# A two-layer encoder trunk in fp32 halves: a changed planner, more load slots, and a new opening with the first norm's weights transposed by PE

## The chip, the core and the metric

The kernel runs on one core of a Trainium2 chip. The metric is the device time of one execution in microseconds. Five engines work side by side, each through its own instructions in order: PE (matrix products and transposes into PSUM), ACT (activations, copies and casts), DVE (elementwise work and reductions), POOL (elementwise work on SBUF only) and SP, which here only issues the DMAs.

## The reference

The input is one sequence of 256 tokens with 1024 features. Two layers follow, each of a SwiGLU feed-forward block, a mixer and a second feed-forward block, every one of them with a norm ahead and a norm behind. All data are fp32.

```python
def rmsnorm(x, g):
    y = x * lax.rsqrt(jnp.mean(x * x, axis=-1, keepdims=True) + EPS)
    return y * g
def swiglu(h, wg, wu, wd):            # 1024 -> 2816 -> 1024
    return (jax.nn.silu(h @ wg) * (h @ wu)) @ wd
for l in range(2):
    g = norm_g[l]
    x = x + 0.5 * rmsnorm(swiglu(rmsnorm(x, g[0]), wg[l, 0], wu[l, 0], wd[l, 0]), g[1])
    h = rmsnorm(x, g[2])
    m = even_mixer(h, ...) if l == 0 else odd_mixer(h, ...)
    x = x + rmsnorm(m, g[3])
    x = x + 0.5 * rmsnorm(swiglu(rmsnorm(x, g[4]), wg[l, 1], wu[l, 1], wd[l, 1]), g[5])
```

The even mixer projects 1024 features to 3368, applies rotary tables, runs 4 differential attention heads and 8 heads that attend to the 64 best of the keys by an indexer's score, and projects back. The odd mixer projects to 3072, runs 16 heads with a bias from a table of clipped distances, and projects back.

## The kernel before

**Tiles.** The tokens are two row blocks of 128, X[0] and X[1] (t = 0 and 1 in the code). Every operand of a matmul is held as a high and a low part in a reduced fp32 type (wh and wl for weights, xTh and xTl for the transposed activations, blk for hidden values), and a product is three matmuls: high by high, high by low and low by high. So each weight that is loaded (tile raw, 512 KB, four slots) is cast by ACT to wh (L267) and reduced by DVE to wl = raw - wh (L269), in pieces of 512 columns.

**Blocks.** A feed-forward block takes its 2816 hidden columns in chunks, one of 256 (tok) and five of 512: gate and up projections into PSUM banks called ps, SiLU on ACT (L532), the product on DVE (L541), transposes by PE (L388), and the down projection into banks called y. A block ends with postnorm: squares of y on ACT (L471), y times g on DVE (L476), the root on POOL (L408, L410), the update of X on DVE (L482). Then prenorm makes the next input: X times g on DVE (L425), squares on ACT (L429), transposes on PE (L388), xTh on ACT (L346), xTl on DVE (L352). The first norm has its own form, prenorm0: X is transposed as it is, and the copies out of PSUM scale by g, which is held as a column per partition (gT), on ACT (L348) and DVE (L354).

**Mixers.** In the even mixer the rotary step takes three DVE operations out of PSUM (L630, L634) and one addition of two SBUF tiles on POOL (L637); the indexer accumulates its scores on DVE (L811) and picks maxima (L818, L819); softmax runs over L705, L709 and L732, the scores' matmuls are L688, the values' L738 to L740. In the odd mixer a table of biases per group of heads comes by DMA (L975).

**Order.** All work is first recorded in a list: every entry has an engine, an estimated time, its inputs and outputs, and a position. Positions follow PE's main stream (pl.pos counts the main matmuls' time); weights stand 9 us ahead of their use (LEAD). Plan.issue then plays an event simulation with these estimates and hands out, for each engine that is free, the ready entry with the lowest position whose buffers are free. The instructions are written in the order in which this hands them out, so a change of an estimate, a slot count or a position moves instructions on all engines. Two rules matter here: an entry with the mark "port" (two SBUF inputs on DVE, or any work of POOL) starts only when the last such one has ended, and its engine stands idle until then (L153 to L156); and a PE entry counts as ready only 0.6 us (SAFE) after its last input from another engine (L164).

**Opening.** SP loads X[0], then g as 1024 single elements (L302), then the first weights and X[1]. Six matmuls of zeros (WARM) keep PE at work until X is there.

## Time and profile before

| | us |
|---|---|
| median of 3 runs | 1026.03 (1025.42 to 1026.78) |
| the profiled execution, its own time | 1024.73 |
| its span | 1022.3 |
| PE busy | 1000.7 (98%) |
| PE weight loads busy | 845.3 (83%) |
| DVE busy | 657.3 (64%) |
| ACT busy | 548.1 (54%) |
| POOL busy | 43.7 (4%) |
| HBM, mean rate over the span | 180 GB/s |

The profile is of one execution; its span runs from the first to the last instruction. A busy PE may run at full clock (2.4 GHz, 1.00 in the rows) or at half (1.2 GHz, 0.50), which the busy time does not tell apart. An idle time is put down to what came last before the instruction behind it.

### The profile page before, as it was taken

The page shows a single profiled execution, that of the slowest core. Times are in us where ns is not written, and L with a number is a line of the kernel's source. Part 1 is how long each engine was busy: PE and PEld are TensorE (multiplying, and loading weights), DVE is VectorE, ACT ScalarE, POOL GpSimd, SP SyncE. Part 2 cuts the span into 40 slices and gives each one's busy share as a digit, 9 for nine tenths or more (in the row PEclk, how much of TensorE's full clock was granted, in tenths as well). Part 3 has the DMA queues.
Part 4 walks back from the last instruction along what each step waited for, and adds up shares of the span by engine and source line. Part 5 has one row for each costly group of instructions (what it writes and reads, how often), then busy time and mean ns, then how long its engine had stood idle before and what let it go on. Part 6 is the DMA issues. An engine that isn't in the chain of part 4 may idle for free.

```text
span 1022.3 us, 14425 instructions
## 1 busy us (share of the span) xinstructions
PE 1000.7 (98%) x5166; PEld 845.3 (83%) x5166; DVE 657.3 (64%) x1299; ACT 548.1 (54%) x1134; POOL 43.7 (4%) x80
## 2 busy tenths in 40 slices
PE   8999999999998999999999999999999989999997
PEld 8888888887876988888888888888899878888886
DVE  6755555689999565545477545557678777555552
ACT  7644444557568454544366444455467756444441
POOL 1000000120200000000010000000000010000000
PEclk8999999999999999999999999999999999999999
DMA  8965665463445476665467666654784347656631
GB/s 286 292 190 181 191 186 163 134 227 105 165 126 163 149 243 185 189 186 198 128 206 246 189 185 187 193 195 147 215 246 155 104 145 230 192 180 194 192 125 41
DMA packets 94151, 185.45 MB, mean 181 GB/s; under 512 B 7040, under 2 KB 29440, under 8 KB 94080
## 3 DMA queue, kind: packets, MB, share of 16 engines
q1 hardware_dynamic: 94080, 184.54, 57.6%
q8 instruction: 40, 0.66, 0.2%
q14 instruction: 31, 0.25, 0.1%
HBM read 183.47 MB, written 1.05 MB: 180 GB/s over the span
## 4 chain that ended last, share of the span: by engine, by line
PE 93%; DVE 3%; ACT 2%; DMA 1%; issue 1%; SPq 0%; POOLq 0%; DVEq 0%; POOL 0%; ACTq 0%
PE ps L378 14%; PE ps L379 14%; PE ps L380 14%; PE y L378 9%; PE y L380 9%; PE y L379 9%; PE ps L370 6%; PE ps L371 5%; PE ps L373 5%; PE ps L388 4%; PE ps L688 1%; DVE wl L269 1%; DMA raw<-in_ow_in_dram 1%; ACT wh L267 1%; DMA raw<-in_wg_dram 0%
## 5 line engine op out<-in xcount | busy, mean ns | idle before, releaser
L269 DVE TENSOR_TENSOR wl<-raw,wh 128x512 fp32r<-128x512 f32 (+1 forms) x664 | 427.6, 684 | 273.2 <-ACT wh L267 272.1
L267 ACT CAST wh<-raw 128x512 fp32r<-128x512 f32 (+1 forms) x664 | 378.6, 617 | 318.6 <-PE ps L380 170.7
L378 PE MATMUL ps<-wh,xTh 128*128 128x512 f32 x592 | 230.4, 389 | 0.0
L380 PE MATMUL ps<-wh,xTl 128*128 128x512 f32 x592 | 230.3, 389 | 0.0
L379 PE MATMUL ps<-wl,xTh 128*128 128x512 f32 x592 | 230.3, 389 | 0.0
L378 PE MATMUL y<-wh,blk 128*128 128x512 f32 x352 | 139.1, 395 | 0.0
L380 PE MATMUL y<-wh,blk 128*128 128x512 f32 x352 | 137.2, 390 | 0.0
L379 PE MATMUL y<-wl,blk 128*128 128x512 f32 x352 | 137.0, 389 | 0.0
L380 PEld LDWEIGHTS ps<-wh,xTl 128*128 128x128 f32 x592 | 111.1, 188 | 23.1
L378 PEld LDWEIGHTS ps<-wh,xTh 128*128 128x128 f32 x592 | 111.1, 188 | 23.0
L379 PEld LDWEIGHTS ps<-wl,xTh 128*128 128x128 f32 x592 | 111.1, 188 | 23.0
L370 PE MATMUL ps<-wh,xTh 128*128 128x512 f32 (+2 forms) x320 | 110.6, 360 | 4.5 <-ACT xTh L346 3.1
L371 PE MATMUL ps<-wl,xTh 128*128 128x512 f32 (+2 forms) x320 | 107.8, 351 | 0.0
L380 PEld LDWEIGHTS y<-wh,blk 128*128 128x128 f32 x352 | 66.1, 188 | 13.9
L379 PEld LDWEIGHTS y<-wl,blk 128*128 128x128 f32 x352 | 66.2, 188 | 13.0
L378 PEld LDWEIGHTS y<-wh,blk 128*128 128x128 f32 x352 | 66.1, 188 | 12.9
L370 PEld LDWEIGHTS ps<-wh,xTh 128*128 128x128 f32 x320 | 62.8, 196 | 12.5 <-ACT xTh L346 3.9
L371 PEld LDWEIGHTS ps<-wl,xTh 128*128 128x128 f32 x320 | 63.1, 197 | 6.1
L373 PE MATMUL ps<-wh,xTl 128*128 128x512 f32 (+2 forms) x320 | 66.5, 347 | 0.0
L388 PE MATMUL ps<-ident,t 128*128 128x128 f32 x386 | 55.9, 273 | 5.7 <-DVE t L425 2.3
L388 PEld LDWEIGHTS ps<-ident,t 128*128 128x128 f32 x386 | 45.5, 140 | 16.2 <-issue 5.6
L373 PEld LDWEIGHTS ps<-wh,xTl 128*128 128x128 f32 x320 | 52.1, 193 | 6.7
(120 smaller groups left out, 938.2 us busy)
## 6 DMA issues: line engine op xcount, KB each, us to landing
raw<-in_wu_dram SPq DMA_DIRECT2D x88, 512.0 KB, 4.3
raw<-in_wd_dram SPq DMA_DIRECT2D x88, 512.0 KB, 3.4
raw<-in_wg_dram SPq DMA_DIRECT2D x86, 512.0 KB, 3.8
raw<-in_ew_in_dram SPq DMA_DIRECT2D x24, 512.0 KB, 4.3
raw<-in_ow_in_dram SPq DMA_DIRECT2D x24, 512.0 KB, 4.6
g<-in_norm_g_dram SPq DMA_DIRECT2D x11, 512.0 KB, 5.1
raw<-in_ew_out_dram SPq DMA_DIRECT2D x8, 512.0 KB, 4.4
raw<-in_ow_out_dram SPq DMA_DIRECT2D x8, 512.0 KB, 3.8
```

The lines of the kernel that those rows point to most:

```text
L267: nc.scalar.copy(ref.t[0][:, sl], raw.t[:, sl])
L269: nc.vector.tensor_sub(ref.t[1][:, sl], raw.t[:, sl], ref.t[0][:, sl].bitcast(F32))
L370: nc.tensor.matmul(o(), ah, bh, start=k == 0, stop=False)
L371: nc.tensor.matmul(o(), ah, bl, start=False, stop=False)
L373: nc.tensor.matmul(o(), al, bh, start=False, stop=k == KT - 1)
L378: nc.tensor.matmul(o, ah, bh, start=start, stop=False)
L379: nc.tensor.matmul(o, ah, bl, start=False, stop=False)
L380: nc.tensor.matmul(o, al, bh, start=False, stop=stop)
L388: nc.tensor.transpose(b.t[:, k * P:(k + 1) * P], s[:, k * P:(k + 1) * P], ident.t)
L688: nc.tensor.matmul(bs[h].t[:, QS[t]], q()[i][rs, bq, t * P:(t + 1) * P], KB.t[j][rs, bk, 0:KL[t]], start=i + j == 0, stop=i == 1)
```

## The change

Six things change.

- Slots: raw has six instead of four; small tiles 14 instead of 16.
- Planner: an entry with the port mark is passed over while the port is taken, so its engine takes other ready work. The 0.6 us of margin for PE is no longer waited for: an entry without margin is only taken if none with margin is ready; entries that take PE's results get the same margin. DMA is estimated at 315 instead of 360 GB/s. An entry may name two engines, and goes to the one that is free first.
- Work that may go to DVE or POOL: the weight subtractions of the even mixer (all projections but the indexer's and the first) and of its output projection, those of the first up projection, and the rotary additions.
- Norms: the work of postnorm and prenorm on ACT and DVE stands 9 us earlier in position. The last down and output projections of each block run column half by column half. Two multiplications of 512 columns behind the differential heads become eight ACT copies of 128.
- Opening, loads: X[0] first half, g as 8 rows of 128 into a tile of the mask, X[0] second half, the first gate weights in four parts, then the up weights and X[1].
- Opening, work: PE transposes g (one matmul, a DVE copy to gT), X[0]'s transposes go to two banks each, copies of X and casts of the first gate weights (now 256 columns each) take turns, the squares of X come behind the copies, and two matmuls of zeros (FILL) follow X[0]'s transposes.

```diff
-SLOTS = {"raw": 4, "w": 8, "xT": 2, "t2": 7, "blk": 8, "g": 2, "pt": 2, "ps": 4, "y": 4, "sm": 16}
+SLOTS = {"raw": 6, "w": 8, "xT": 2, "t2": 7, "blk": 8, "g": 2, "pt": 2, "ps": 4, "y": 4, "sm": 14}
-LAT = {"PE": 0.2, "ACT": 0.14, "DVE": 0.13, "POOL": 0.17, "DMA": 2.0}
+LAT = {"PE": 0.2, "ACT": 0.14, "DVE": 0.13, "POOL": 0.17, "DMA": 2.2}
-WARM = 6
+WARM, FILL = 6, 2
...
+                    if o["port"] and port > now + 1e-9:
+                        fits = False
+                        event(port, "", None)
...
-                    if fits:
+                    if fits and o["safe"] <= now + 1e-9:
                         got = o
                         break
+                    if fits and late is None:
+                        late = z
...
-                    d["ready"] = max(d["ready"], end + (OWN[e] if d["eng"] == (e,) else o["lat"] + (SAFE if d["eng"] == ("PE",) else 0.0)))
+                    at = end + (OWN[e] if d["eng"] == (e,) else o["lat"])
+                    d["ready"] = max(d["ready"], at)
+                    if d["eng"] == ("PE",) != (e,):
+                        d["safe"] = max(d["safe"], at + SAFE)
...
-            self.step = 512 if self.per * b % 512 == 0 else b
+            self.step = 512 if self.per * b % 512 == 0 and (pool or first is None) else b
...
-                op(DVE, n_dve(self.step), lo, r=[rk, (ref, i, 0)], w=[(ref, i, 1)], pos=q + 0.05, port=True)
+                op(DVE + POOL if self.pool else DVE, {"DVE": us, "POOL": 0.1 + self.step * 0.00245} if self.pool else us, lo,
+                   r=[rk, (ref, i, 0)], w=[(ref, i, 1)], pos=q + 0.05, port=True)
...
-    op(DMA, 0.1, lambda: nc.sync.dma_start(gT.t, norm_g[0, 0].rearrange("(k p) -> p k", p=P)), w=[gT], pos=-99.5)
+    op(DMA, 0.1, lambda: nc.sync.dma_start(cmask.t[0:KT, 0:P], norm_g[0, 0].rearrange("(k p) -> k p", p=P)), w=[cmask], pos=-100)
+    op(PE, 0.11, lambda: nc.tensor.transpose(bb.t[:, P:P + KT], cmask.t[0:KT, 0:P], ident.t[0:KT, 0:KT]), r=[cmask, ident], w=[bb], pos=-90)
+    op(DVE, 0.08, lambda: nc.vector.tensor_copy(gT.t, bb.t[:, P:P + KT]), r=[bb], w=[gT], pos=-90)
...
+        first = pos - LEAD
...
+        pos = pl.pos - LEAD
...
+        order = [(k, t, n) for k in range(kn) for t in ts for n in range(2)]
+        if last:
+            order.sort(key=lambda o: o[2])
...
-        op(POOL, 0.11 + n * 0.00218, lambda: nc.gpsimd.tensor_add(a.t[:, :n], a.t[:, :n], r.t[:, :n]),
+        op(DVE + POOL, {"DVE": n_dve(n), "POOL": 0.11 + n * 0.00218}, add, r=[(r, 0), (r, 1)], w=[a], port=True)
...
-            op(DVE, n_dve(512), scl, r=[(ss, 4), oA[t]], w=[(jk, h) for h in range(4)], pos=pn)
+                op(ACT, n_act(P, True, 1), scl, r=[(ss, 4), oA[t]], w=[(jk, h)], pos=pn)
```

The order at the opening, on SP (loads). X0 and X1 are the row blocks, raw the weights' slots. Before:

```order
L291 DMA X0_72<-in_x_dram 128x512 x2
L302 DMA gT_74<-in_norm_g_dram 128x8x1
L259 DMA raw_2_106<-in_wg_dram 128x2x256
L291 DMA X1_73<-in_x_dram 128x512 x2
L259 DMA raw_2_106<-in_wg_dram 128x2x256
```

And now:

```order
L303 DMA X0_72<-in_x_dram 128x512
L315 DMA cmask_75<-in_norm_g_dram 8x128
L303 DMA X0_72<-in_x_dram 128x512
L269 DMA raw_2_107<-in_wg_dram 128x2x256 x2
L269 DMA raw_5_119<-in_wg_dram 128x2x256 x2
L269 DMA raw_12_142<-in_wu_dram 128x2x256 x2
L303 DMA X1_73<-in_x_dram 128x512 x2
```

X1's two loads stood behind the first of the weights' loads and stand behind the sixth now.

The order at the opening, on ACT (xTh are copies out of PSUM, wh weight casts, t2 the squares of X). Before:

```order
L454 ACTIVATE t2_4_113,sm_3_112<-X0_72 128x512
L454 ACTIVATE t2_5_117,sm_3_112<-X0_72 128x512
L348 ACTIVATE xTh_8_131<-ps_6_120,gT_74 128x128
L267 CAST wh_10_135<-raw_2_106 128x512
L348 ACTIVATE xTh_8_131<-ps_6_120,gT_74 128x128 x3
L348 ACTIVATE xTh_8_131<-ps_7_126,gT_74 128x128 x4
L267 CAST wh_10_135<-raw_2_106 128x512
```

And now:

```order
L365 ACTIVATE xTh_8_129<-y_3_113,gT_74 128x128
L365 ACTIVATE xTh_8_129<-y_4_114,gT_74 128x128 x2
L277 CAST wh_10_138<-raw_2_107 128x256 x2
L365 ACTIVATE xTh_8_129<-y_3_113,gT_74 128x128
L277 CAST wh_10_138<-raw_2_107 128x256 x2
L365 ACTIVATE xTh_8_129<-y_6_123,gT_74 128x128
L277 CAST wh_14_160<-raw_5_119 128x256
L365 ACTIVATE xTh_8_129<-y_7_124,gT_74 128x128
L277 CAST wh_14_160<-raw_5_119 128x256
```

The squares have moved behind the copies, and each later copy has a cast of half the size behind it.

The order on POOL where the even mixer begins (t2 tiles are rotary results). Before:

```order
L637 TENSOR_TENSOR t2_332_1912<-t2_332_1912,t2_335_1923 128x288
L783 COPY t2_332_1912<-t2_332_1912 128x96
L637 TENSOR_TENSOR t2_336_1935<-t2_336_1935,t2_339_1953 128x512
L637 TENSOR_TENSOR t2_359_2044<-t2_359_2044,t2_360_2048 128x288
L783 COPY t2_359_2044<-t2_359_2044 128x96
```

And now:

```order
L816 COPY t2_339_1942<-t2_339_1942 128x96
L279 TENSOR_TENSOR wl_355_2021<-raw_323_1854,wh_354_2020 128x512
L279 TENSOR_TENSOR wl_358_2031<-raw_331_1897,wh_357_2030 128x512
L670 TENSOR_TENSOR t2_362_2054<-t2_362_2054,t2_365_2061 128x288
L279 TENSOR_TENSOR wl_364_2059<-raw_338_1928,wh_363_2058 128x512
L816 COPY t2_362_2054<-t2_362_2054 128x96
L279 TENSOR_TENSOR wl_376_2100<-raw_361_2046,wh_375_2099 128x512
```

Weight subtractions have come to POOL, 35 in the whole program, and of ten rotary additions three are left there, two of 512 columns and one of 288.

The order on ACT where the even mixer hands over to the feed-forward block (y tiles are the mixer's output, X0 the updated row block, xTh the next input). Before:

```order
L471 ACTIVATE t2_617_3350,sm_616_3349<-y_531_2943 128x512
L471 ACTIVATE t2_618_3355,sm_616_3349<-y_534_2952 128x512
L267 CAST wh_621_3370<-raw_606_3287 128x512 x2
L471 ACTIVATE t2_624_3379,sm_623_3378<-y_554_3041 128x512
L429 ACTIVATE t2_626_3383,sm_625_3382<-X0_72 128x512
L429 ACTIVATE t2_628_3387,sm_625_3382<-X0_72 128x512
L267 CAST wh_630_3391<-raw_613_3318 128x512 x2
L471 ACTIVATE t2_634_3409,sm_623_3378<-y_559_3057 128x512
L346 CAST xTh_635_3412<-ps_632_3396 128x4x128
```

And now:

```order
L500 ACTIVATE t2_622_3372,sm_621_3371<-y_550_3020 128x512
L500 ACTIVATE t2_625_3386,sm_621_3371<-y_557_3040 128x512
L500 ACTIVATE t2_628_3399,sm_627_3398<-y_582_3158 128x512
L277 CAST wh_629_3405<-raw_603_3257 128x512 x2
L447 ACTIVATE t2_632_3411,sm_631_3410<-X0_72 128x512
L447 ACTIVATE t2_634_3415,sm_631_3410<-X0_72 128x512
L500 ACTIVATE t2_637_3424,sm_627_3398<-y_585_3174 128x512
L363 CAST xTh_640_3436<-ps_636_3419 128x4x128
```

The two casts that stood between the squares of X0 and the copy to xTh are gone from there.

## Rows read from the trace of the kernel before

**Rows 1.** The page's busy times: share of the span and number of instructions of each engine.

```profile
PE 1000.7 (98%) x5166; PEld 845.3 (83%) x5166; DVE 657.3 (64%) x1299; ACT 548.1 (54%) x1134; POOL 43.7 (4%) x80
```

**Rows 2.** Busy time of each engine in stretches of 20 us, with the granted clock of PE (1.00 is 2.4 GHz), the share of the DMA engines and GB/s.

```profile
0.00:20.00 20.00, 16.25 (x92) 15.24 (x93) 12.25 (x32) 14.92 (x39) 3.54 (x13) 0.83 0.88 274
...
200.00:220.00 20.00, 19.29 (x108) 16.76 (x107) 18.02 (x41) 12.54 (x25) 4.55 (x8) 1.00 0.72 240
...
240.00:260.00 20.00, 18.11 (x114) 14.05 (x113) 19.68 (x77) 12.00 (x36) 0.00 (x0) 1.00 0.35 108
...
300.00:320.00 20.00, 19.34 (x124) 16.09 (x123) 19.04 (x67) 17.68 (x51) 0.00 (x0) 1.00 0.53 156
320.00:340.00 20.00, 16.37 (x94) 14.17 (x93) 16.36 (x31) 10.70 (x28) 4.52 (x8) 0.91 0.60 192
...
740.00:760.00 20.00, 18.45 (x148) 17.70 (x148) 14.52 (x40) 12.51 (x32) 0.89 (x3) 0.91 0.85 269
...
820.00:840.00 20.00, 17.41 (x107) 14.99 (x106) 16.60 (x31) 11.87 (x29) 4.50 (x8) 1.00 0.54 168
```

**Rows 3.** The same in two stretches of the opening; the figure behind POOL's is the granted clock.

```profile
8.00:10.00 2.00, 1.54 (x8) 1.04 (x6) 1.83 (x7) 2.00 (x7) 0.00 (x0) 0.65 1.04 368
...
14.00:16.00 2.00, 2.00 (x13) 2.00 (x13) 2.00 (x6) 2.00 (x6) 0.00 (x0) 0.64 0.78 237
```

**Rows 4.** The timeline of the opening: start, duration (of a run of like instructions their whole time), engine, line, operation, and the idle time before it with what ended it.

```profile
5.17 0.35 ACT L348 ACTIVATE xTh<-ps,gT 128x128 fp32r<-128x128 f32 x1
...
6.32 0.62 ACT L267 CAST wh<-raw 128x512 fp32r<-128x512 f32 x1 [0.80 <-DMA raw<-in_wg_dram]
6.84 1.91 ACT L348 ACTIVATE xTh<-ps,gT 128x128 fp32r<-128x128 f32 x7
...
6.99 1.37 PE L388 MATMUL ps<-ident,X 128*128 128x128 f32 x8 [1.47 <-DMA X<-in_x_dram]
...
7.75 0.87 DVE L354 SCALAR_TENSOR_TENSOR xTl<-ps,gT,xTh 128x128 fp32r<-128x128 f32 x3
...
8.77 0.55 PE L370 MATMUL ps<-wh,xTh 128*128 128x256 f32 x1 [0.41 <-ACT xTh L348]
...
10.66 0.55 PE L370 MATMUL ps<-wh,xTh 128*128 128x256 f32 x1 [0.70 <-DVE xTl L354]
...
12.93 2.48 DVE L269 TENSOR_TENSOR wl<-raw,wh 128x512 fp32r<-128x512 f32 x4
```

**Rows 5.** Busy times, as in rows 2, around the longest wait of the even mixer.

```profile
236.00:250.00 14.00, 12.11 (x70) 9.06 (x69) 13.75 (x44) 8.38 (x23) 0.65 (x1) 1.00 0.41 127
```

**Rows 6.** The timeline of the even mixer: a POOL addition beside DVE work, the indexer's accumulation on DVE without and with a POOL addition beside it, and PE's longest wait.

```profile
220.78 2.21 POOL L637 TENSOR_TENSOR t<-t,t 128x512 f32<-128x512 f32 x1 [0.36 <-DVE t L634]
...
229.07 0.34 DVE L811 SCALAR_TENSOR_TENSOR t<-t,wI,cmask 128x128 f32<-128x128 f32 x1
229.29 1.29 POOL L637 TENSOR_TENSOR t<-t,t 128x512 f32<-128x512 f32 x1 [6.30 <-DVE t L634]
229.44 1.28 DVE L811 SCALAR_TENSOR_TENSOR t<-t,wI,t 128x128 f32<-128x128 f32 x1
...
248.16 0.55 PE L388 MATMUL ps<-ident,t 128*128 128x128 f32 x3 [1.63 <-DVE blk L354]
```

**Rows 7.** The timeline where the even mixer hands over to the feed-forward block.

```profile
320.85 3.09 DVE L269 TENSOR_TENSOR wl<-raw,wh 128x512 fp32r<-128x512 f32 x5
...
324.76 0.50 PE L380 MATMUL y<-wh,xTl 128*128 128x512 f32 x1 [1.09 <-DVE xTl L352]
...
330.22 1.13 ACT L267 CAST wh<-raw 128x512 fp32r<-128x512 f32 x2
...
332.45 0.39 PE L370 MATMUL ps<-wh,xTh 128*128 128x256 f32 x1 [1.43 <-ACT xTh L346]
```

**Rows 8.** Busy times and granted clock, as in rows 2, behind the waits at 332 and at 749 us.

```profile
332.00:336.00 4.00, 3.55 (x18) 3.55 (x19) 3.68 (x8) 0.89 (x2) 1.47 (x4) 0.61 0.57 148
...
749.00:752.00 3.00, 3.00 (x17) 3.00 (x17) 2.65 (x15) 2.72 (x10) 0.31 (x1) 0.55 1.05 278
752.00:755.00 3.00, 3.00 (x25) 3.00 (x25) 1.89 (x4) 1.85 (x5) 0.31 (x1) 0.88 1.00 322
```

**Rows 9.** The odd mixer: busy times of two stretches, as in rows 2 (the last two figures are the share of the DMA engines and GB/s).

```profile
724.00:728.00 4.00, 4.00 (x19) 3.30 (x19) 2.37 (x4) 3.02 (x6) 0.00 (x0) 1.00 0.00 0
...
740.00:744.00 4.00, 4.00 (x35) 4.00 (x35) 1.85 (x3) 2.28 (x4) 0.27 (x1) 1.00 0.99 346
```

**Rows 10.** The chain that ended last, at the load of the odd mixer's weights (start, duration).

```profile
738.80 7.06 DMA raw<-in_ow_in_dram
```

**Rows 11.** PE's waits in the timeline, in the odd mixer and where it hands over to the feed-forward block.

```profile
747.12 0.33 PE L688 MATMUL ps<-KBh,blk 64*128 64x128 f32 x2 [1.03 <-ACT KBh L346]
...
827.23 1.23 PE L388 MATMUL ps<-ident,t 128*128 128x128 f32 x8 [1.16 <-DVE t L425]
...
829.89 0.39 PE L370 MATMUL ps<-wh,xTh 128*128 128x256 f32 x1 [1.43 <-ACT xTh L346]
```

**Rows 12.** The timeline of the tail: PE's last matmul, the last square and the last update.

```profile
1015.85 0.39 PE L380 MATMUL y<-wh,blk 128*128 128x512 f32 x1
...
1016.27 0.60 ACT L471 ACTIVATE t<-y 128x512 f32<-128x512 f32 x1
...
1017.90 1.54 DVE L482 SCALAR_TENSOR_TENSOR X<-t,sm,X 128x512 f32<-128x512 f32 x3 [0.21 <-POOL sm L410]
```

More of the change, by code (lines that the diff above doesn't have):

```diff
@@ L124, in issue @@
                     continue
-                skip, got = [], None
+                skip, got, late = [], None, None
                 while heap[e]:
@@ L137, in issue @@
                             event(q.used[1], "", None)
-                    if fits:
+                    if fits and o["safe"] <= now + 1e-9:
                         got = o
                         break
+                    if fits and late is None:
+                        late = z
                     skip.append(z)
+                if got is None and late is not None:
+                    got = late[2]
+                    skip.remove(late)
                 for z in skip:
@@ L149, in issue @@
                     q.t = q.make()
-                us = o["us"]
-                o["fn"]()
-                start = now
+                us = o["us"] if len(o["eng"]) == 1 else o["us"][e]
+                o["fn"]() if len(o["eng"]) == 1 else o["fn"](e)
                 if o["port"]:
-                    start = max(start, port)
-                    port = start + us
-                end = eng[e] = o["end"] = start + us
+                    port = now + us
+                end = eng[e] = o["end"] = now + us
                 todo -= 1
@@ L425, in mg @@
                     nc.vector.tensor_mul(xn[h].t, X[t].t[:, HS[h]], g.t[:, HS[h]])
-                op(DVE, n_dve(512), mg, r=[(X[t], h), (g, h)], w=[xn[h]], pos=pos - 0.01, port=True)
+                op(DVE, n_dve(512), mg, r=[(X[t], h), (g, h)], w=[xn[h]], pos=first - 0.01, port=True)
             q = t2() if late else xn[h]
@@ L488, in down, with f @@
     def down(ts, unit, kn, lhs, lk, y, kt0, first, last):
[L490 to L497 removed]
+        order = [(k, t, n) for k in range(kn) for t in ts for n in range(2)]
+        if last:
+            order.sort(key=lambda o: o[2])
+        for k, t, n in order:
+            wk, w = unit.part(k, n * 512, (n + 1) * 512)
+            def f(n=n, k=k, w=w, t=t):
+                mm3(y[t][n].t, tuple(z[:, kt0 + k, t * P:(t + 1) * P] for z in lhs()), w(),
+                    first and k == 0, last and k == kn - 1)
+            main(0.68, f, r=wk + lk(t), w=[y[t][n]])
     last_silu = [None]
```

91 lines of the change are left out of this document (48 added, 43 removed).

## The prediction

> **What bounds the kernel now.** I read the page's first line before anything else: PE is busy for 1000.7 of the span's 1022.3 us [rows 1], so only what PE loses can move the end. Next the busy time in stretches of 20 us [rows 2]: the feed-forward stages fill PE and are left out there; the losses sit in the opening (3.75 us idle in 0 to 20), in the even mixer (0.71, 1.89 and 0.66 in three stretches), where it hands over to the next feed-forward block (3.63 in 320 to 340), in the odd mixer (1.55 in 740 to 760) and at its handover (2.59 in 820 to 840). The rest of the idle time is the tail behind the last matmul and two gaps below half a microsecond. Last the granted clock, which the busy time hides: it is 2.4 GHz nearly everywhere, but 1.2 GHz in the opening from about 8.6 to 15.4 us (a mean of 0.65 over 8 to 10 is 1.4 us at half, 0.64 over 14 to 16 the same) [rows 3], and for some 3.4 us each after the waits at 332 and 749 [rows 8]. At half clock PE counts as busy and does half the work, so 3.4 us there lose 1.7 us.
>
> **The change part by part.** I count gains against the profiled execution (1024.73 us, 2.43 above its span); its median is 1.30 higher, and I carry the difference over.
>
> Opening. The load of the first norm's weights shrinks from 1024 elements of 4 bytes to 8 rows, X's second row block and its load go behind the first weights, and casts of X and of weights alternate. The first scaled copy of X was at 5.17 [rows 4]; it still needs four transposes, and now one more on PE and a DVE copy, so I leave it there. A copy of 128 columns takes ACT 0.27 (1.91 for 7) and DVE 0.29 (0.87 for 3); a weight cast of 512 columns takes 0.62 on either (0.62; 2.48 for 4), so I put one of 256 at 0.33, half and a little [rows 4]. Eight copies and eight casts are 4.8 us on ACT and 5.0 on DVE, which starts one copy later: done at about 10.7. PE follows them from about 6.6 on (5.17, three copies, a cast, the low part's subtraction; the first weights had landed by 6.32 even behind the small elements), so by 10.7 it has run the first 16 weight matmuls, against 5 before, when it waited 0.41 and 0.70 and got going at 10.66 [rows 4]. That is 11 matmuls, 0.21 us each at 1.2 GHz, 2.3 us; but eight transposes of X's second block, which before were done (1.37 us, within an idle stretch) now stand in the stream. Net 0.9. I take 0.7. Upper end: if the earlier matmuls and the two filling ones keep the clock up, the 6.8 us at half clock go, 3.4. Lower end: thinner work before 10.7 puts the rise of the clock off by one stretch like those of rows 8, so -1.7 + 0.7 = -1.0. Casts and loads cannot limit PE after that: the 0.5 MB of X are moved behind 1.5 MB of weights, and PE wants X's second block only after 24 matmuls.
>
> Here the Trainium skill speaks against the change: its page TensorE: Matmul & The Clock Gate (Part 4, PE-mode transpose) says that transposes do not count as PE work for the clock. By that, the transposes now in the stream would put the rise off, and the opening would give -1.0; the trace agrees so far as the clock fell at 8.6 right behind the transposes of 6.99, but they also followed a wait of 1.47 [rows 4].
>
> Even mixer. DVE is the second engine here: 13.75 busy of 14 us around PE's longest wait, 1.63 at 248.16 [rows 5, 6]. By the program's order 35 weight subtractions (0.62 each) leave DVE for POOL, 21.7 us; seven rope additions come back, at most 4.2; two scalings go to ACT, where time is free. So DVE loses about 17 us of work in a stage of 120. But a POOL addition of two tiles takes 1.29, and DVE work on two SBUF tiles beside it waits: an accumulation of 0.34 took 1.28; the other way round POOL took 2.21 [rows 6]. The planner now lets neither start while the other holds the port and takes other work instead. The waits of this stage sum to 3.26 [rows 2]; I take 1.0 of it, between all of it and a loss of 3 (below): a relief that is real, on a path which PE waits for only now and then.
>
> Even to feed-forward. Before, five weight subtractions (3.09 us) stood ahead of the last head's low part, for which PE waited 1.09 [rows 7]. Now three do: two less, 1.2 us earlier. Against it, the last output projection runs its column halves one after the other, so one more group (three matmuls of 512 columns, 0.68) stands behind the wait ahead of the second half's square: 0.5 left. Then two casts (1.13 at 330.22) stood ahead of ACT's copy of the new X, for which PE waited 1.43 [rows 7]; they are now behind it: 1.0, not all, since the square of the second row block stays ahead. With both waits cut by more than half I expect the clock to hold, as it did at 820 to 840 with 2.59 us of waits [rows 2, 11]: another 1.7 [rows 8]. Term 3.2, bounds 0 and 4.2 (1.09 + 1.43 + 1.7).
>
> Odd mixer. PE waits 1.03 at 747.12 [rows 11] for a copy that comes late because the weights do: their load took 7.06 us [rows 10] at a saturated queue (0.99 busy, 346 GB/s), some 12 us after a stretch of 4 in which nothing was moved [rows 9]. Four raw slots were full then. Six let two more loads of 0.5 MB into the idle stretch, 3 us of transfer at that rate; in the order 18 projection loads now stand ahead of the first bias load, 16 before. The 1.55 idle [rows 2] and the clock's 1.7 [rows 8] should go: 3.2 at most, none at least; I take 2.8, as the bias tables use the same queue.
>
> Odd to feed-forward. Waits of 1.16 and 1.43 [rows 11], clock up [rows 2]. One more group of 0.68 now follows the first row block's last matmul, and covers that much of the first. On ACT one cast has gone ahead of the copy and one is still there: nothing. Term 0.7, bounds 0 and 2.6.
>
> Tail. The last square starts 0.03 us behind the end of PE, then POOL, then the update at 1017.90 [rows 12]. Halves one after the other let the first square run early, but the second one was not waiting for it: nothing, within 0.1.
>
> Unchanged work in the feed-forward blocks is covered by PE; norm steps that move ahead of casts there cost nothing while weights are cast with the planner's lead of 9 us. Sum: 0.7 + 1.0 + 3.2 + 2.8 + 0.7 = 8.4. Every engine's order is new, so I set one wait like that of 248.16 (1.63) against it: 6.8. Against the median: 1026.03 - 6.8 = 1019.2.
>
> **The rivals.** *The port.* POOL holds it 35 times for 1.29 us, 45 us of the stage's 120. If DVE stands behind it as often as it did with the additions (the two collisions of rows 6 lose 0.9 each), half of 38 POOL instructions (three additions stay) cost DVE 17 us, all that it gained, and at worse places: PE waits, say, six times more for 1.3 and the clock falls twice (3.4). That is 11 us, which eats the other terms' 7.4 and leaves 1029. It decides from about 8 us lost. Beside this, the Trainium skill's SBUF — State Buffer (Who interferes with whom) calls the shared ports an exclusive lock: the second one waits for the whole instruction; the rows at 229 us agree [rows 6]. For it: DVE was 98% busy. Against: the planner knows the port now. *The clock stays the same.* The waits shrink but not enough; both falls and the opening's remain, and the two 1.7 do not come: 1019.2 + 3.4 = 1022.6. For it: the falls came after waits of 1 to 2.5 us, which I only cut. *All of it.* Opening at full clock (2.7 more), mixer waits gone (2.3), no new wait (1.6): 1012.6. *It doesn't do what it says.* New waits take back what the old ones gave: 1026.
>
> **How the numbers follow.** Forecast 1019.2 (gain 4.5 to 9.5): 0.50. Clock the same, 1021.5 to 1024: 0.18. All of it, 1010 to 1016: 0.14. Nothing gained, 1024 to 1028: 0.11. Port, above 1028: 0.07. The range from 1012 to 1026 leaves out the far half of the last two and the best of the third, under 2 in 10. 0.2% is 2.05 us, about what a measurement can tell from no change: faster means below 1024.0, 0.81; same 0.12; slower 0.07.
>
> **What would show it.** Opening: first weight matmul near 6.6 us, 16 by 10.7, and the granted clock of 8 to 16 us. Even mixer: DVE's busy time in 200 to 320 lower by 10 or more, no DVE work on two SBUF tiles above 1 us. Handover at about 330: both waits under 1 us and no half clock. Odd mixer: data moved where the queue was idle, no wait near 747. Wrong, if PE waits anew in the even mixer for more than 4 us, or if the clock falls at places where it held.

## The result and the profile after

The changed kernel takes 1020.04 us (median of 4 runs, 1018.78 to 1020.28), the kernel before on the same chips 1025.72 (1024.22 to 1026.78): a ratio of 0.9948, interval 0.9934 to 0.9962, or 5.7 us less. The profiled execution took 1018.78, its span 1017.0, 5.3 less than before. It is the shortest of the four: the others took 1.2 to 1.5 longer, at a mean granted clock of 0.994 or 0.993 where it had 0.995. Where their clock was lower is not on record, so what is read below from its trace can hold one fall of the clock less than the median does. Its busy times, to be held against [rows 1]:

```profile
PE 999.8 (98%) x5171; PEld 843.8 (83%) x5171; DVE 651.4 (64%) x1274; ACT 549.4 (54%) x1146; POOL 88.1 (9%) x108
```

PE does the same work, POOL twice as much. Stretches of 20 us that answer to [rows 2] (columns as there: window, sum, PE, its weight loads, DVE, ACT, POOL, granted clock, DMA share, GB/s):

```profile
0.00:20.00 20.00, 18.16 (x110) 16.11 (x111) 12.12 (x37) 15.65 (x44) 2.33 (x11) 1.00 0.93 331
...
220.00:240.00 20.00, 18.30 (x126) 14.06 (x124) 19.29 (x27) 10.50 (x21) 12.47 (x9) 1.00 0.47 143
240.00:260.00 20.00, 18.46 (x95) 14.65 (x96) 16.63 (x73) 10.80 (x34) 6.29 (x5) 0.83 0.40 132
...
280.00:300.00 20.00, 18.90 (x115) 15.12 (x114) 16.81 (x47) 16.54 (x56) 10.92 (x8) 1.00 0.40 129
...
320.00:340.00 20.00, 18.36 (x113) 15.92 (x113) 18.59 (x35) 13.99 (x34) 4.41 (x8) 1.00 0.60 185
...
700.00:720.00 20.00, 19.02 (x92) 15.67 (x92) 16.72 (x28) 12.06 (x27) 4.65 (x5) 1.00 0.78 262
...
740.00:760.00 20.00, 20.00 (x176) 19.47 (x175) 15.64 (x47) 14.09 (x37) 0.85 (x3) 1.00 0.89 291
...
820.00:840.00 20.00, 18.40 (x125) 16.38 (x124) 12.91 (x25) 10.38 (x25) 3.66 (x6) 1.00 0.35 119
```

The opening now runs at full clock, the odd mixer's wait near 747 is gone, and the handovers at 320 and 820 wait less. But in the even mixer PE has new idle time (1.70 in 220 to 240, where there was none, and 1.10 in 280 to 300) and half clock in 240 to 260, and 700 to 720 has an idle microsecond that it did not have.

Windows of equal time don't hold equal work any more, so I cut both traces where work is equal: at the last output matmul of a block. PE's timeline (start, duration) of the kernel before, for the first feed-forward block, the even mixer, the second feed-forward block and the odd mixer (the tail's is in [rows 12]):

```profile
198.17 0.39 PE L380 MATMUL y<-wh,blk 128*128 128x512 f32 x1
...
328.30 0.39 PE L380 MATMUL y<-wh,xTl 128*128 128x512 f32 x1
...
520.84 0.39 PE L380 MATMUL y<-wh,blk 128*128 128x512 f32 x1
...
825.68 0.39 PE L380 MATMUL y<-wh,xTl 128*128 128x512 f32 x1
```

The same five of the changed kernel, the tail's with them:

```profile
196.30 0.39 PE L397 MATMUL y<-wh,blk 128*128 128x512 f32 x1
...
329.20 0.39 PE L397 MATMUL y<-wh,xTl 128*128 128x512 f32 x1
...
519.37 0.39 PE L397 MATMUL y<-wh,blk 128*128 128x512 f32 x1
...
821.11 0.39 PE L397 MATMUL y<-wh,xTl 128*128 128x512 f32 x1
...
1010.27 0.39 PE L397 MATMUL y<-wh,blk 128*128 128x512 f32 x1
```

The differences between these rows make five stretches; the third and fourth feed-forward blocks begin with the handover behind the second block and the odd mixer.

| stretch | before | after | difference | predicted |
|---|---|---|---|---|
| opening and first block | 198.17 | 196.30 | -1.87 | -0.7 |
| even mixer | 130.13 | 132.90 | +2.77 | -1.5, with one new wait of +1.6 set against the sum |
| handover and second block | 192.54 | 190.17 | -2.37 | -2.7 |
| third block and odd mixer | 304.84 | 301.74 | -3.10 | -2.8 |
| handover and fourth block | 190.17 | 189.16 | -1.01 | -0.7 |
| tail | 6.45 | 6.73 | +0.28 | 0 |
| span | 1022.30 | 1017.00 | -5.30 | -6.8 |

(The handover term of 3.2 is split: 0.5 of it is a stall that lies inside the even mixer's stretch.) The four stretches with a gain came near the forecast or better. The even mixer went the other way, by 4.3. Its whole stretch, before and then now (columns as above):

```profile
198.17:328.30 130.13, 125.35 (x740) 102.84 (x738) 123.30 (x340) 85.86 (x218) 17.65 (x20) 1.00 0.52 170
...
196.30:329.20 132.90, 128.09 (x739) 105.14 (x738) 117.30 (x308) 87.02 (x225) 57.82 (x48) 0.97 0.52 162
```

PE is idle for 4.78 before and for 4.81 now, so the waits have changed places but not their sum. Nearly all of the 2.77 is time in which PE is busy, at a lower clock. The longest wait now in the timeline (as in rows 6), with what ran ahead of it:

```profile
229.78 9.56 POOL L279 TENSOR_TENSOR wl<-raw,wh 128x512 fp32r<-128x512 f32 x7 [6.87 <-ACT wh L277]
...
232.40 1.78 DVE L670 TENSOR_TENSOR t<-t,t 128x512 f32<-128x512 f32 x1
...
234.10 1.38 DVE L844 SCALAR_TENSOR_TENSOR t<-t,wI,t 128x128 f32<-128x128 f32 x1
...
236.83 3.45 DVE L844 SCALAR_TENSOR_TENSOR t<-t,wI,t 128x128 f32<-128x128 f32 x4
...
240.81 0.68 DVE L369 TENSOR_TENSOR KBl<-ps,KBh 128x512 fp32r<-128x512 f32 x1
...
241.54 0.32 PE L721 MATMUL ps<-KBh,blk 64*128 64x128 f32 x1 [2.91 <-DVE KBl L369]
```

POOL subtracts seven times in one go. Every DVE instruction with two SBUF inputs in that time is stretched: an accumulation that takes 0.34 alone [rows 6] takes 1.38, four take 3.45, a rotary addition 1.78. DVE work with an input from PSUM is not: a rotary product (L662) takes 0.75 at 230.43, beside POOL, and 0.73 at 224.58, with nothing on POOL. KBl (0.68) starts when POOL's run is over, but it stands behind the stretched accumulations and a weight subtraction, and PE waits 2.91 for it. Then the clock falls (windows of 2 us, last figures as above):

```profile
242.00:244.00 2.00, 2.00 (x10) 1.58 (x9) 1.93 (x9) 0.05 (x1) 0.00 (x0) 0.50 0.92 280
244.00:246.00 2.00, 2.00 (x14) 1.35 (x13) 1.90 (x13) 1.81 (x8) 0.00 (x0) 0.50 1.03 387
246.00:248.00 2.00, 2.00 (x8) 1.49 (x7) 1.83 (x12) 0.00 (x0) 0.00 (x0) 0.50 0.30 115
```

Three windows at 1.2 GHz lose 3 us of work, which no idle time shows.

### The profile page after: what moved, and what is told of

It reads as the page before. It is cut to its first block, busy times and chain, and to the rows that moved or that the text cites. A ratio compares the mean times of both kernels' runs of the same rounds, so it can differ in the third digit from the quotient of the medians.

```text
span 1017.0 us, 14500 instructions
## 1 busy us (share of the span) xinstructions
PE 999.8 (98%) x5171; PEld 843.8 (83%) x5171; DVE 651.4 (64%) x1274; ACT 549.4 (54%) x1146; POOL 88.1 (9%) x108
## 4 chain that ended last, share of the span: by engine, by line
PE 93%; DVE 4%; ACT 2%; issue 1%; POOLq 0%; DVEq 0%; POOL 0%; ACTq 0%
PE ps L395 15%; PE ps L397 15%; PE ps L396 15%; PE y L395 9%; PE y L397 9%; PE y L396 9%; PE ps L390 5%; PE ps L387 5%; PE ps L388 5%; PE ps L405 4%; PE ps L721 2%; DVE wl L279 1%; ACT wh L277 1%; DVE t L844 1%; PE ps L771 0%
## 5 line engine op out<-in xcount | busy, mean ns | idle before, releaser
L279 DVE TENSOR_TENSOR wl<-raw,wh 128x512 fp32r<-128x512 f32 (+2 forms) x633 | 406.8, 685 | 263.3 <-ACT wh L277 262.8
L277 ACT CAST wh<-raw 128x512 fp32r<-128x512 f32 (+2 forms) x668 | 377.6, 615 | 296.0 <-PE ps L397 181.4
L397 PEld LDWEIGHTS ps<-wh,xTl 128*128 128x128 f32 x592 | 111.1, 188 | 23.1
L425 POOL TENSOR_TENSOR sm<-sm 128x1 f32<-128x1 f32 x24 | 16.5, 687 | 783.3 <-ACT t L500 733.8
```

What stands on the lines that cost most here:

```text
L277: nc.scalar.copy(ref.t[0][:, sl], raw.t[:, sl])
L279: (nc.vector if e == "DVE" else nc.gpsimd).tensor_sub(ref.t[1][:, sl], raw.t[:, sl], ref.t[0][:, sl].bitcast(F32))
L397: nc.tensor.matmul(o, al, bh, start=False, stop=stop)
L425: op(POOL, 0.27, lambda: nc.gpsimd.tensor_add(s.t[:, 2:3], s.t[:, 2:3], s.t[:, 1:2]), r=[(s, 1)], w=[(s, 2)], pos=pos)
```

## The experiments

The first theory is that POOL's weight subtractions hold the port that DVE needs. Its rival is that the planner's new order puts KBl late. The other terms of the prediction each have a run that takes one part of the change back. Twelve kernels ran. This table has them all, each ratio against the kernel before on the same chip. The stretches are from one profiled execution each, cut as above.

| run | median | ratio (interval) | to first block | even mixer | second block | third block and odd mixer | fourth block |
|---|---|---|---|---|---|---|---|
| before | 1025.72 | 1 | 198.17 | 130.13 | 192.54 | 304.84 | 190.17 |
| changed | 1020.04 | 0.9948 (0.9934 to 0.9962) | 196.30 | 132.90 | 190.17 | 301.74 | 189.16 |
| e1_no_pool | 1015.48 | 0.9908 (0.9883 to 0.9934) | 196.31 | 129.59 | 191.64 | 301.74 | 189.20 |
| e2_no_subs | 1013.27 | 0.9890 (0.9868 to 0.9912) | 196.29 | 127.06 | 191.66 | 301.75 | 189.16 |
| e3_rope_pool | 1014.41 | 0.9899 (0.9877 to 0.9920) | 196.45 | 128.51 | 190.12 | 301.75 | 189.16 |
| e4_pool_copy | 1010.75 | 0.9866 (0.9844 to 0.9888) | 196.06 | 124.73 | 190.13 | 301.74 | 189.17 |
| e5_raw4 | 1017.22 | 0.9912 (0.9887 to 0.9938) | 196.31 | 130.27 | 190.17 | 301.77 | 189.25 |
| e6_fill0 | 1021.35 | 0.9951 (0.9933 to 0.9968) | 197.99 | 132.96 | 190.17 | 301.74 | 189.22 |
| e7_no_sort | 1022.32 | 0.9973 (0.9959 to 0.9988) | 196.29 | 130.74 | 191.55 | 305.75 | 189.03 |
| e8_no_lead | 1018.67 | 0.9922 (0.9895 to 0.9948) | 196.44 | 133.37 | 190.08 | 301.70 | 189.15 |
| e9_old_dma | 1020.84 | 0.9938 (0.9914 to 0.9962) | 196.97 | 134.09 | 190.17 | 301.74 | 189.21 |
| e10_old_rules | 1031.05 | 1.0058 (1.0038 to 1.0077) | 195.91 | 142.11 | 192.06 | 301.86 | 189.73 |
| e11_all_dve | 1015.15 | 0.9881 (0.9852 to 0.9910) | 196.30 | 128.70 | 190.13 | 301.74 | 189.16 |
| e12_before_raw6 | 1019.09 | 0.9966 (0.9941 to 0.9991) | 196.75 | 129.73 | 191.06 | 301.05 | 191.67 |

### The even mixer: who does the subtractions

**e1_no_pool**, edits to the changed kernel:

```diff
-            self.src, self.b, self.cuts, self.pool, self.first = src, b, cuts, pool, first
+            self.src, self.b, self.cuts, self.pool, self.first = src, b, cuts, False, first
...
-        op(DVE + POOL, {"DVE": n_dve(n), "POOL": 0.11 + n * 0.00218}, add, r=[(r, 0), (r, 1)], w=[a], port=True)
+        op(POOL, 0.11 + n * 0.00218, lambda: add("POOL"), r=[(r, 0), (r, 1)], w=[a], port=True)
```

> The changed kernel, with all weight subtractions on DVE and all ten rotary additions on POOL as before the change; the rest of the change stays. Theory of the port: in the changed kernel POOL ran seven subtractions in one go (9.56 us), DVE's accumulations of 0.34 took 1.4 beside them, PE waited 2.91 us for KBl and its clock was at half for some 7 us. Without the subtractions on POOL the wait falls under 1.7, the clock holds, and the stretch from 200 to 320 us gives back about 4.6: 1015.4. Rival, the order: the planner's new order puts KBl late, and 21.7 us of subtractions come back to a DVE that is 95% busy: the wait stays or grows, 1020 to 1024.

The total is as the port's theory had it (1015.48). In the profiled execution the even mixer gives back 3.3 of the 4.6, and the second block is 1.5 longer: the clock fell in the handover there. That execution took 1017.01, and the other three 1015.33 to 1015.57 at a higher mean clock (0.998 or 0.999 where it had 0.997), so the fall is not a mark of this kernel.

**e2_no_subs**, the first of the two edits alone:

```diff
-            self.src, self.b, self.cuts, self.pool, self.first = src, b, cuts, pool, first
+            self.src, self.b, self.cuts, self.pool, self.first = src, b, cuts, False, first
```

> The changed kernel, with the weight subtractions on DVE alone; the rotary additions may still go to either engine (five go to DVE). Theory of the port: as without both, 1015 to 1016.5, since it was the run of subtractions that held the port. Rival, the rotary additions: two of the three waits in the even mixer stood behind an addition on DVE (1.10 and 0.33), so these stay and the gain is 1.4 smaller than without both. Rival, the order: 1020 to 1024.

1013.27, below what the theory had, the lowest median with the full computation and ahead of the changed kernel (the intervals are apart). The even mixer takes 127.06, 5.8 less, though 35 subtractions are back on DVE. The rival of the rotary additions falls: there is no wait for one.

**e3_rope_pool**, the second edit alone:

```diff
-        op(DVE + POOL, {"DVE": n_dve(n), "POOL": 0.11 + n * 0.00218}, add, r=[(r, 0), (r, 1)], w=[a], port=True)
+        op(POOL, 0.11 + n * 0.00218, lambda: add("POOL"), r=[(r, 0), (r, 1)], w=[a], port=True)
```

> The changed kernel, with the weight subtractions where the planner puts them (POOL mostly) and all rotary additions on POOL. Theory of the port: POOL has seven two-input operations more on top of the subtractions, so the even mixer loses as much as in the changed kernel or more: 1020 to 1023, with DVE accumulations above 1 us. Rival, the rotary additions: the waits for additions on DVE go, 1018.5.

Both were wrong: 1014.41. The planner gave POOL 24 subtractions here instead of 35, and they met other DVE work. The collisions are there all the same (timeline of this run):

```profile
241.91 6.49 POOL L279 TENSOR_TENSOR wl<-raw,wh 128x512 fp32r<-128x512 f32 x5 [8.35 <-ACT wh L277]
...
245.88 1.28 DVE L899 SCALAR_TENSOR_TENSOR sm<-sm,nlam,sm 128x2 f32<-128x2 f32 x1
...
249.67 3.93 POOL L279 TENSOR_TENSOR wl<-raw,wh 128x512 fp32r<-128x512 f32 x3 [1.27 <-ACT wh L277]
...
252.40 2.40 DVE L904 SCALAR_TENSOR_TENSOR t<-t,sm,t 128x128 f32<-128x128 f32 x4
...
253.80 0.83 PE L405 MATMUL ps<-ident,t 128*128 128x128 f32 x3 [2.26 <-DVE t L904]
```

An instruction of two columns took 1.28 us at 245.88, and PE waited 2.26 behind stretched work. So what a collision costs PE depends on where it falls, and a new order moves that by several us. Runs with different orders can't price the port; the next one keeps the order.

**e4_pool_copy:**

```diff
-                    (nc.vector if e == "DVE" else nc.gpsimd).tensor_sub(ref.t[1][:, sl], raw.t[:, sl], ref.t[0][:, sl].bitcast(F32))
+                    nc.gpsimd.tensor_copy(ref.t[1][:, sl], raw.t[:, sl]) if e == "POOL" else nc.vector.tensor_sub(ref.t[1][:, sl], raw.t[:, sl], ref.t[0][:, sl].bitcast(F32))
```

> The changed kernel in exactly its own order, but POOL's weight operation copies raw to wl instead of subtracting wh from it (the low parts of these weights are left out of the result). One input in place of two, the same place and the same engine. Theory that the port is held by POOL work with two SBUF inputs: DVE's accumulations beside it are back at 0.34 us, PE's wait of 2.91 goes to under 1, the clock holds, 1015 to 1016. Rival, any POOL work holds it: accumulations stay above 1 us and the time stays in proportion to POOL's duration, 1018 to 1020. Rival, the order alone: the wait stays at 2.9 although the accumulations are short, 1020.

With the same order on every engine the even mixer takes 124.73, 8.2 less than in the changed kernel, and from 202 to 320 us PE has no wait for DVE. So the order alone is not the cause: it costs nothing once POOL's instructions are short. The total, 1010.75, is lower than any of the three theories had it. Groups of the changed kernel from 190 to 330 us (count, busy, mean ns, idle before):

```profile
L279 POOL TENSOR_TENSOR wl<-raw,wh 128x512 fp32r<-128x512 f32 x35 | 47.6, 1387 | 43.4 <-ACT wh L277 31.9 <-DVE sm L738 11.5
...
L670 DVE TENSOR_TENSOR t<-t,t 128x512 f32<-128x512 f32 x6 | 6.8, 1128 | 0.1
L844 DVE SCALAR_TENSOR_TENSOR t<-t,wI,t 128x128 f32<-128x128 f32 x7 | 4.7, 678 | 0.2
```

and of the run with copies:

```profile
L279 POOL CAST wl<-raw 128x512 fp32r<-128x512 f32 x35 | 23.5, 700 | 34.0 <-PE ps L388 21.6 <-issue 11.4 <-POOL wl L279 0.8
...
L670 DVE TENSOR_TENSOR t<-t,t 128x512 f32<-128x512 f32 x6 | 4.9, 822 | 0.1
L844 DVE SCALAR_TENSOR_TENSOR t<-t,wI,t 128x128 f32<-128x128 f32 x7 | 3.1, 437 | 0.2
```

The additions shrink from 1128 to 822 ns, the accumulations from 678 to 437, not quite to the 349 of the run without subtractions. The mean hides two kinds. Three accumulations ran beside copies (timeline of this run), the other four with nothing on POOL:

```profile
227.44 1.85 POOL L279 CAST wl<-raw 128x512 fp32r<-128x512 f32 x3 [0.21 <-PE ps L388]
227.59 1.84 DVE L844 SCALAR_TENSOR_TENSOR t<-t,wI,t 128x128 f32<-128x128 f32 x3
```

Beside a copy an accumulation takes 0.51 to 0.61 (0.57 on average), about as long as the copy (0.62); the four others take 0.34. Beside a subtraction of 1.39 one took 1.38. So work of POOL with one SBUF input holds DVE too, as the rival had it, but only for its own half length. What the second input does apart from making POOL's instruction longer is not shown: the 8.2 are for a shorter instruction that also does not wait for the cast wh.

**e11_all_dve**, the first edit and the additions on DVE:

```diff
-        op(DVE + POOL, {"DVE": n_dve(n), "POOL": 0.11 + n * 0.00218}, add, r=[(r, 0), (r, 1)], w=[a], port=True)
+        op(DVE, n_dve(n), lambda: add("DVE"), r=[(r, 0), (r, 1)], w=[a], port=True)
```

> The changed kernel with all weight subtractions and all rotary additions on DVE, so that POOL has no large two-input work left. Beside the kernel without subtractions on POOL (even mixer 127.06, 1013.3) DVE has 3.1 us more of its own and no collision at the port. Theory of the port: every collision costs about what an addition costs, so the even mixer takes 126 to 127: 1012.5 to 1013.3. Rival, the load of DVE: it was busy for 19.5 of every 20 us there, so 3.1 more come out at the end: 129 to 130, 1016.

The even mixer takes 128.70, 1.6 more than with five additions on POOL: the rival's direction, about half its size. That a few additions on POOL pay is not shown by this: the order is another one, and against the kernel before the two are equal (0.9881 here, 0.9890 with five additions on POOL, and the intervals overlap for most of their width). The second block held its clock in the profile here (190.13) and not in that one (191.66).

**e10_old_rules**, the planner as it was:

```diff
-                    if o["port"] and port > now + 1e-9:
+                    if False:
...
-                if o["port"]:
-                    port = now + us
-                end = eng[e] = o["end"] = now + us
+                start = max(now, port) if o["port"] else now
+                port = start + us if o["port"] else port
+                end = eng[e] = o["end"] = start + us
...
-                        d["safe"] = max(d["safe"], at + SAFE)
+                        d["ready"] = max(d["ready"], at + (SAFE if d["eng"] == ("PE",) else 0.0))
```

> The changed kernel with the planner's old rules: an entry with the port mark makes its engine stand until the port is free, and the margin of 0.6 us is waited for by every PE entry. Theory of the rules: they brought the odd mixer's 2.0 (its block back to 117.6) and part of the handovers' (blocks behind the mixers 0.5 to 1 longer); the even mixer stays near 132.9 as POOL still has the subtractions: 1022 to 1024. Rival, the loads: the odd mixer's block stays at 115.6, and the total within 1 of 1020.

Slower than before the change, with the even mixer at 142.11: with the old rules POOL was handed 44 subtractions in this stretch, and PE lost both time and clock there (a window of this run):

```profile
280.00:300.00 20.00, 15.42 (x94) 12.81 (x93) 17.44 (x64) 15.40 (x53) 8.90 (x6) 0.69 0.36 106
```

So the two new rules together are worth 9.2 in the even mixer once POOL subtracts, in the one order that each kernel has. At the handovers the two waits sum to 2.12 here at either place, to 1.64 and 1.60 in the changed kernel: 0.5 each. The second block is 1.9 longer (192.06) because the clock fell there as well, the fourth, where it held, 0.6 (189.73). The odd mixer does not need the rules.

### The opening: the two filling matmuls

**e6_fill0:**

```diff
-WARM, FILL = 6, 2
+WARM, FILL = 6, 0
```

> The changed kernel without the two filling matmuls behind the transposes of X's first row block; nothing else moves by the order. Theory: they keep PE at work while it waits for the first weights, and the clock at 2.4 GHz; without them it falls to half in 6 to 15 us as before the change, and the opening loses about 2 us (most of that stretch PE follows ACT and DVE anyway): 1022. Rival: the earlier start of the weight matmuls keeps the clock up by itself, and nothing is lost: 1020.

1.69 lost to the end of the first block in the profiled execution; of the opening's 1.87 only 0.18 is left. The totals can't tell the two kernels apart (0.9951 and 0.9948, and the seven executions run from 1019.07 to 1022.42), but the clock can: from 9 to 15 us it is 1.00 in all eleven profiled kernels with the two matmuls and 0.50 in this one. Two windows of this run:

```profile
9.00:11.00 2.00, 1.93 (x7) 1.66 (x7) 2.00 (x8) 2.00 (x7) 0.00 (x0) 0.50 1.04 360
...
13.00:15.00 2.00, 2.00 (x11) 2.00 (x10) 0.62 (x2) 1.18 (x4) 0.15 (x1) 0.50 1.05 408
```

and the same two of the changed kernel:

```profile
9.00:11.00 2.00, 1.65 (x7) 1.04 (x8) 2.00 (x8) 2.00 (x7) 0.00 (x0) 1.00 1.05 364
...
13.00:15.00 2.00, 2.00 (x16) 1.76 (x16) 1.84 (x5) 2.00 (x6) 0.16 (x1) 1.00 1.05 409
```

### The handovers: halves and lead

**e7_no_sort:**

```diff
-            order.sort(key=lambda o: o[2])
+            pass
```

> The changed kernel, the last down and output projections of each block not column half by column half but as before. Theory of the prediction: one group of 0.68 less behind the wait at each handover: 0.7 lost at odd to feed-forward, 0.5 to 0.7 at even to feed-forward, 1021.3. Rival: the waits at the handovers end with the last square of the second row block whatever the order of the halves, 1020. Rival: without the halves the wait at the even handover grows so much that the clock falls, 1.7 more: 1023.

All three missed the place. At the fourth block nothing is lost (189.03). At the second the waits are the same and the clock fell, 1.4. The large loss, 4.0, lies ahead of the odd mixer, half of it a longer wait and half a lower clock behind it (0.67 from 708 to 712 us; DVE and PE in the timeline of this run):

```profile
699.35 6.71 DVE L279 TENSOR_TENSOR wl<-raw,wh 128x512 fp32r<-128x512 f32 x11 [0.23 <-ACT wh L277]
...
708.03 1.32 PE L405 MATMUL ps<-ident,t 128*128 128x128 f32 x8 [2.97 <-DVE t L453]
```

Eleven weight subtractions went ahead of the next norm's scaling (L453). In the changed kernel it is five:

```profile
700.15 3.10 DVE L279 TENSOR_TENSOR wl<-raw,wh 128x512 fp32r<-128x512 f32 x5 [0.23 <-ACT wh L277]
...
707.73 0.50 PE L387 MATMUL ps<-wh,xTh 128*128 128x512 f32 x1 [0.97 <-ACT xTh L363]
```

In this order the halves save a wait that the rest of the change would have made; 0.97 of it is left, where before there was 0.29.

**e8_no_lead:**

```diff
-        first = pos - LEAD
+        first = pos
...
-        pos = pl.pos - LEAD
+        pos = pl.pos
```

> The changed kernel, the work of postnorm and prenorm on ACT and DVE at its old position instead of 9 us earlier. Theory of the prediction: casts and subtractions stand ahead of it again at the even handover, xTh comes 1.0 later, and with the longer waits the clock falls as before the change, 1.7: 1022.7. Rival: what cut these waits is the order of the column halves alone, and the norms' position does nothing: 1020.

The rival: every stretch but the even mixer is within 0.2 of the changed kernel's. By itself the norms' lead of 9 us gains nothing.

### The odd mixer: slots, loads, or order

**e5_raw4:**

```diff
-SLOTS = {"raw": 6, "w": 8, "xT": 2, "t2": 7, "blk": 8, "g": 2, "pt": 2, "ps": 4, "y": 4, "sm": 14}
+SLOTS = {"raw": 4, "w": 8, "xT": 2, "t2": 7, "blk": 8, "g": 2, "pt": 2, "ps": 4, "y": 4, "sm": 14}
```

> The changed kernel with four raw slots again instead of six. Theory of the prediction: the six slots let the odd mixer's loads into the idle queue; with four, PE waits about 1.5 us again near 745 and the clock falls behind it for 3.4 us: the stretch from 740 to 760 loses 3.2, 1023. Rival: the new positions of the loads alone have removed that wait; nothing changes there, 1020. The even mixer may move by a few us either way, as its order changes too; it is read apart.

301.77, as with six: the slots are not needed for this gain. Nor do they pay in the changed kernel as a whole: with four the total is 1017.22, the ratio 0.9912 against 0.9948 with intervals that hardly touch, and the even mixer, in another order, is 2.6 shorter.

**e9_old_dma:**

```diff
-LAT = {"PE": 0.2, "ACT": 0.14, "DVE": 0.13, "POOL": 0.17, "DMA": 2.2}
+LAT = {"PE": 0.2, "ACT": 0.14, "DVE": 0.13, "POOL": 0.17, "DMA": 2.0}
...
-                op(DMA, f * 512 / cuts / 315e3, load, w=[(raw, i)],
+                op(DMA, f * 512 / cuts / 360e3 + 0.02, load, w=[(raw, i)],
```

> The changed kernel with the planner's old estimates for loads (360 GB/s, 2.0 us latency). The odd mixer's gain did not come from the six slots, since with four the block's time stayed at 115.67. Theory of the loads: the slower estimate makes the planner hand out loads and the work behind them in another order, so KBh is no longer late; with the old one the wait near 745 and the half clock come back, and the odd mixer's block goes from 115.6 to 117.6: 1022. Rival, the planner's rules: the block stays at 115.6, 1020.

301.74 again. No single part is needed, so the last run asks which is enough.

**e12_before_raw6**, the kernel before with

```diff
-SLOTS = {"raw": 4, "w": 8, "xT": 2, "t2": 7, "blk": 8, "g": 2, "pt": 2, "ps": 4, "y": 4, "sm": 16}
+SLOTS = {"raw": 6, "w": 8, "xT": 2, "t2": 7, "blk": 8, "g": 2, "pt": 2, "ps": 4, "y": 4, "sm": 14}
```

> The kernel before the change with six raw slots (and 14 small tiles, to make room) and nothing else of the change. Taking the slots, the loads' estimate, the halves, the norms' lead or the planner's rules back from the changed kernel one at a time left the odd mixer without its wait near 745. Theory of the slots, in a weaker form: they are enough by themselves, though something else of the change is enough too; the wait of 1.03 near 747 goes, the clock holds there, and from the end of the third feed-forward block to the end of the odd mixer it takes 115.6 to 116.5 instead of 117.6. Rival: the slots do nothing there, and it is the order that the rest of the change gives on ACT and PE; 117.6 stays. The even mixer may shift as well, and is read apart.

The slots (with the two small tiles less) are enough in the profiled execution: 301.05, 0.7 better than the whole change, since the wait of 0.97 at the odd mixer's start does not come. Its window, beside the one of [rows 2] with 18.45 at 0.91:

```profile
740.00:760.00 20.00, 20.00 (x177) 19.13 (x176) 16.35 (x51) 13.51 (x37) 1.32 (x4) 1.00 0.86 272
```

In this execution it also saves 1.4 in the opening, where the clock was back at 1.00 by 11 us, and 1.5 in the second block, where it held behind waits as long as before (1.08 and 1.45), and loses 1.5 in the fourth, where it fell. This one line is worth 0.9966, and its interval overlaps that of the whole change; its ten executions run from 1017.42 to 1028.23.

## Why the prediction was right, and where it was not

**The sum** was 6.8, and the medians give 5.7. It held because misses cancel: the four stretches that gain gave 8.35 (1.87 + 2.37 + 3.10 + 1.01) where I had 6.9, the even mixer lost 2.77 where I had a gain of 1.5, and the new wait of 1.6 that I had set against the sum paid for part of that. That the total came out near the forecast is in part luck, with the clock too: 1.5 of the gain at the first handover is a clock that held there in the profiled execution and fell in three other kernels behind the same waits.

**Opening.** PE's timeline of the changed kernel has the first weight matmul and the 16th where the working had them (6.6 and 10.7):

```profile
6.54 0.38 PE L387 MATMUL ps<-wh,xTh 128*128 128x256 f32 x1
...
10.85 0.39 PE L388 MATMUL ps<-wl,xTh 128*128 128x256 f32 x1
```

But the run without fill had the same rows and gained 0.18, not 0.7: the early start alone brings little. I put that down to PE following ACT and DVE until 11 us; no run separates it. The gain is the clock, which I had as the upper end (3.4) and priced at twice what it brought: 1.7. The kernel before with six slots points the same way: with the old opening, but the clock at 1.00 again by 11 us, it gained 1.42. The clock stayed at 1.00 with the transposes of X's second block in the stream, so the loss of 1.0 that I had from the rule of the Trainium skill (TensorE: Matmul & The Clock Gate, Part 4, PE-mode transpose: transposes don't count as work for the clock) did not come. That does not speak against the rule: these are two groups of four transposes, 0.60 each, between weight matmuls. The run without fill agrees with it: from 4.0 to 6.5 us PE had nothing but transposes and a wait of 0.66, and the clock fell at about 9.

**Even mixer: the step that failed.** I put a relief of 1.0, because DVE loses 17 us of work and the planner knows the port. The first half held in part: from 200 to 320 us DVE is busy for 105.7 us where it was 114.7, 9 less and not 17. Cut at equal work it is 6.0 less (117.30 for 123.30), and 15.4 less in the same order with copies (107.91): the rest is DVE's work stretched. The second did not hold. The planner keeps the two apart in its own time, but the program holds no wait for the port, and POOL's seven subtractions ran in one go beside DVE's accumulations. What the rival of the port said came true, in one place instead of six: a wait of 2.91 and one fall of the clock, 4.3 worse than the forecast where the rival had 11. My own signs of being wrong came up too: PE's waits of 0.48, 0.33, 2.91 and 1.10 are all new and sum to 4.82, and the clock fell where it had held. In the same order with copies of half the length the stretch is 8.2 shorter. The page SBUF — State Buffer (Who interferes with whom) of the Trainium skill calls the port an exclusive lock; the traces agree, down to an instruction of two columns that took 1.28.

**Even to feed-forward.** 2.37 against 2.7, and the stall of 1.09 at 324.76 [rows 7] is gone. Of the two waits behind it the second fell from 1.43 [rows 7] to 0.54. The first did not move, where I had both under 1 us. Before:

```profile
329.79 1.23 PE L388 MATMUL ps<-ident,t 128*128 128x128 f32 x8 [1.11 <-DVE t L425]
```

and now:

```profile
330.69 1.23 PE L405 MATMUL ps<-ident,t 128*128 128x128 f32 x8 [1.10 <-DVE t L443]
...
332.47 0.39 PE L387 MATMUL ps<-wh,xTh 128*128 128x256 f32 x1 [0.54 <-ACT xTh L363]
```

So 0.9 of the gain is shorter waits and 1.5 the clock, which held in this execution. I had expected it to hold because the waits are shorter. The runs don't bear that out: behind the same two waits it fell in three kernels, and in the run with six slots it held behind waits as long as before. The casts that stood ahead of the norm's copy are indeed behind it, but not by the norms' lead: without that the gain stays. With the old rules the second wait is 1.38 again, though the first is down to 0.74.

**Odd mixer.** 3.10 against 2.8. That slots can do it is shown by the run that adds them alone. That they do it in the changed kernel is not: without them the gain stays. Which other part is enough too remains open, since lead, halves, estimate and rules were each taken back alone. The way I had it, two more loads moved while the queue was idle, is not in the traces. Beside [rows 9], the changed kernel:

```profile
724.00:728.00 4.00, 4.00 (x19) 3.34 (x18) 3.41 (x6) 4.00 (x8) 0.00 (x0) 1.00 0.20 53
```

and from 720 to 724 it moves 7 GB/s, where before it was 135; the run with six slots alone has a stretch of 4 us with nothing moved as well, from 720 to 724. What is earlier is KBh's copy: it starts at 742.66 now and at 746.49 before, 3.8 sooner, of which 1.5 were won ahead of the third block.

**Odd to feed-forward.** 1.01 against 0.7, from 1.16 and 1.43 [rows 11] to:

```profile
822.24 1.23 PE L405 MATMUL ps<-ident,t 128*128 128x128 f32 x8 [0.74 <-DVE t L443]
...
824.33 0.38 PE L387 MATMUL ps<-wh,xTh 128*128 128x256 f32 x1 [0.86 <-ACT xTh L363]
```

Not by the halves, as I had it (without them 189.03), but again partly by the rules (189.73 without).

**Tail.** 0.28 longer, all of it behind the start of the last update (from 1012.31 to 1017.0 now, from 1017.90 to 1022.3 before [rows 12]), where the output is stored; the cause is open.

One correction to the section on the change: the planner's margin of 0.6 us is for PE entries with inputs from other engines, and for these alone; work that takes PE's results has none.

## What to carry to other kernels

Work handed to POOL is not off DVE where DVE works on two SBUF tiles beside it: such an instruction waited here for POOL's, whether that read two tiles or one, so a long one on POOL costs most. A planner that keeps the two apart in its own time does not keep them apart on the chip (putting in waits was not tried). Change one part of such a planner's tables at a time and read the result by stretches of equal work, since a total hides a loss of 4 us behind four gains, and every edit moves the order elsewhere by as much. When several parts remove the same wait, undoing each shows that none is needed; adding one to the old kernel shows which is enough.

## What was not expected of the hardware

- The clock after a handover is a matter of the run: with waits of about 1.1 and 0.5 us there it fell in three kernels (second block 191.55 to 191.66) and held in seven (190.1 to 190.2); with 1.16 and 1.42 at 820 it fell in the run with six slots (fourth block 191.67) and held before the change (190.17). A fall costs 1.4 to 1.5 each time. What decides it was not found.
- Two matmuls on zeros in the opening decided whether PE ran at 2.4 or at 1.2 GHz from 9 to 15 us, and were worth 1.7.
- A one-input copy on POOL is not free for DVE either: three accumulations beside such copies (0.62 us each) took 0.57 us on average, the four without 0.34.
